# A hybrid decoder trunk: the attention of the first layer with VectorE and ScalarE, too, in a written order

## The chip, the core and the metric

The kernel runs on one core of a Trainium2 chip. The metric is the time of one execution on the device, in microseconds (us), as the median of several runs. TensorE does the matrix products, VectorE (DVE) and ScalarE (ACT) read their results out of PSUM, GpSimd (POOL) works on SBUF, and SyncE (SP) issues the DMA transfers.

## The reference

A trunk of two layers over 1024 tokens of width 1024, in float32. Layer 0, which the change touches, is

```python
h = rmsnorm(x, attn_norm[0])
q_a, k_a, v_a, q_b, k_b, v_b = split(h @ w_in)
o_a = stick_breaking_attention(q_a, k_a, v_a)          # 8 heads x 64, strictly causal
o_b = sliding_window_attention(q_b, k_b, v_b, sinks, rel_bias_table)   # 8 q heads, 2 kv heads, window 128
x = x + concat(o_a, o_b) @ w_out
x = x + swiglu(rmsnorm(x, ffn_norm[0]), ...)
```

In stick-breaking attention a weight is `exp(log_beta + between)`, where `between` is a reversed cumulative sum of `log_sigmoid(-z)` over the keys; the kernel forms it as a running product of `sigmoid(-z)` along reversed keys, and the weights are its differences, which it moves into the values. In sliding-window attention the scores get a relative bias and each head a sink, and a softmax follows. Layer 1 has latent attention and the same kind of feed-forward block; a final normalisation ends the trunk.

## The kernel before

Everything is kept as transposed tiles of 128 features by 512 tokens; `hf` names the half of the tokens. A float32 operand is split into a high part (`hi`, rounded by a ScalarE cast) and the rest (`lo`, a VectorE subtraction), and a product is three matrix products (`mm3`). Weights come through `stream`: `take()` returns a unit, and sees to it that the next one is loaded (DMA into `wa`) and split (`whi` on ScalarE, `wlo` on VectorE, four buffers each), a whole unit of up to two tiles at a time.

`layer0_attention` projects the first pair of stick-breaking heads, and then calls `weave`, which interleaves eight segments with filler. The first four segments are the four pairs of stick-breaking heads (20 slots each), the other four the pairs of sliding-window heads (8 slots each). A slot holds, in this order of emission:

- `part`: transposes of two blocks of weights into a PSUM bank `t` (two buffers), and their split into `pth` (ScalarE) and `ptl` (VectorE);
- the scores that the slot two ahead needs (`AHEAD`): the product into a bank `z`; then for stick-breaking a sigmoid on ScalarE into `w` and a scan on VectorE (L683, L685), for sliding-window a bias addition (L589) and a maximum (L591) on VectorE and two exponentials on ScalarE (L593), after GpSimd has put the sink beside them (L588);
- filler: quarters of the projections of the next pair (`unit_items`: 24 products in four parts, evacuated by VectorE into `ev` at L507 and then stacked by `stack_q`, `stack_k` or turned into value tokens by `sb_values` and `v_tokens`), the rows of the relative bias, and in the last four segments the early output projection (`early_out`, L835) with its reloads. How much of it a slot takes is its share of the segment's weight; it is used up one slot before the segment's end;
- the product with the values (`pv`, bank `o`) of the slot before, and, where a group of blocks ends, `end`: a copy of half the bank (`otmp`, ScalarE) and additions on VectorE (L725, L626).

At the end of a half, sliding-window outputs are multiplied by the reciprocal sums (`normalise`: a transpose, a copy `rrow`, a round trip through memory, a GpSimd multiplication at L331), and `done` stores the split output (`spill`: cast L312, GpSimd subtraction L313, two DMAs). `early_out` reads the stick-breaking outputs back (`early_act`, L827). The bias rows of a pair of sliding-window heads are read (L574) when its first block is scored.

Who sets the order: the block of `weave` stands in

```python
with self.tc.manual_schedule(engines={mybir.EngineType.PE}):
```

so TensorE executes it as it is written. The instructions of VectorE, ScalarE, GpSimd and SyncE are ordered by a planner that simulates the program, with its own costs. Every engine takes its instructions in the order so found and waits on semaphores for what is not ready.

## Time and profile before

| | before |
|---|---|
| median of three runs | 2510.03 us (2509.27 to 2511.41) |
| profiled execution | 2502.03 us, span 2500.3 us |
| granted TensorE clock, mean | 0.972 |
| busy: TensorE, VectorE, ScalarE, GpSimd | 93%, 77%, 49%, 39% of the span |
| stick-breaking part of the weave | 63.8 to 351.4 us, TensorE busy 263.54 us |
| sliding-window part | 351.4 to 493.0 us, TensorE busy 128.15 us |

In a row of the timeline stand the start, the duration, the engine, the line, the operation with output and inputs by their names, and in brackets the idle time of that engine before it with what ended it. A row of the waits has the engine and line that waited, what it waited for, the total in us, the number of times and the longest.

### The profile page before, as it was taken

What the parts mean: (1) busy time and instruction counts of PE and PEld (TensorE: products, weight loads), DVE (VectorE), ACT (ScalarE), POOL (GpSimd) and SP (SyncE); (2) the same over time, 40 slices, a digit from 0 to 9 for tenths busy, and PEclk for the clock granted to TensorE, in tenths of its full rate; (3) what the DMA queues carried; (4) which work ended last, traced back from release to release, by engine and by line L of the source; (5) the groups of instructions that cost most, each with busy time, mean ns of one, the idle gap of its engine ahead of it and who ended that gap; (6) DMA issues with size and microseconds to landing.
All of it is one profiled execution on the core that took longest, in us unless ns stands there. A gap on an engine that the chain in (4) does not pass through costs nothing. (4 is left out here: it accounts for less than half of the span.)

```text
span 2500.3 us, 33743 instructions
## 1 busy us (share of the span) xinstructions
PE 2334.6 (93%) x11252; PEld 1913.9 (77%) x11252; DVE 1912.7 (77%) x2864; ACT 1237.0 (49%) x2469; POOL 979.4 (39%) x786
## 2 busy tenths in 40 slices
PE   7999999888999999899987999999989999998996
PEld 4777787776788888678766888887768888886784
DVE  6777776779676667799977888885588766678988
ACT  5555555554233334344655787774453333343453
POOL 5333232216975354343222323321047544533333
PEclk9999999999999999999998999999989999999998
DMA  3011225543444234453333111135225433345531
GB/s 119 26 43 39 68 99 192 189 171 122 141 137 140 88 107 151 145 171 123 121 115 95 50 62 60 53 133 195 90 96 183 146 105 102 107 129 170 169 103 71
DMA packets 161931, 289.22 MB, mean 116 GB/s; under 512 B 20091, under 2 KB 28764, under 8 KB 161756
## 3 DMA queue, kind: packets, MB, share of 16 engines
q1 hardware_dynamic: 161756, 287.05, 35.1%
q8 instruction: 89, 1.46, 0.2%
q14 instruction: 86, 0.70, 0.1%
HBM read 207.19 MB, written 79.27 MB: 115 GB/s over the span
## 5 line engine op out<-in xcount | busy, mean ns | idle before, releaser
L145 ACT CAST whi<-wa 128x512 fp32r<-128x512 f32 (+1 forms) x422 | 255.8, 607 | 473.3 <-PE mm L231 118.8
L146 DVE TENSOR_TENSOR wlo<-wa,whi 128x512 fp32r<-128x512 f32 (+1 forms) x422 | 334.0, 792 | 63.9 <-ACT whi L145 62.2
L177 POOL TENSOR_TENSOR wa<-s,wa 128x512 f32<-128x512 f32 (+1 forms) x68 | 97.0, 1426 | 327.1 <-DVE wlo L146 297.8
L195 POOL TENSOR_TENSOR s<-wb,wb 128x512 f32<-128x512 f32 (+1 forms) x68 | 104.6, 1538 | 161.6 <-DVE wlo L146 146.2
L146 DVE TENSOR_TENSOR wlo<-wb,whi 128x512 fp32r<-128x512 f32 (+1 forms) x136 | 136.2, 1001 | 33.3 <-ACT whi L145 33.2
L1424 PE MATMUL z<-mk,mq 128*128 128x512 f32 (+2 forms) x576 | 148.1, 369 | 11.2 <-ACT w L1437 10.4
L145 ACT CAST whi<-wb 128x512 fp32r<-128x512 f32 (+1 forms) x136 | 82.3, 605 | 142.3 <-PE a L231 43.6
L230 PE MATMUL mm<-hh,whi 128*128 128x512 f32 x312 | 129.0, 413 | 1.7 <-ACT whi L145 1.7
L1437 ACT ACTIVATE w<-z,st 128x512 f32<-128x512 f32 (+3 forms) x192 | 110.9, 583 | 35.3 <-DVE st L1433 25.4
L231 PE MATMUL mm<-hl,whi 128*128 128x512 f32 x312 | 125.6, 403 | 0.0
L177 POOL TENSOR_TENSOR wa<-wa,wa 128x512 f32<-128x512 f32 (+1 forms) x68 | 100.0, 1471 | 65.3 <-issue 52.0
L232 PE MATMUL mm<-hh,wlo 128*128 128x512 f32 x312 | 125.4, 402 | 0.0
L1430 DVE TENSOR_REDUCE st<-z 128x1 f32<-128x512 f32 (+1 forms) x192 | 104.2, 550 | 26.8 <-PE z L1424 19.1
L391 DVE TENSOR_TENSOR ptl<-t,pth 128x512 fp32r<-128x512 f32 x160 | 108.2, 684 | 18.2 <-ACT pth L390 13.5
L927 POOL TENSOR_TENSOR c<-c,c 128x512 f32<-128x512 f32 x66 | 99.3, 1518 | 43.1 <-DVE c L1031 37.1
L1424 PEld LDWEIGHTS z<-mk,mq 128*128 128x128 f32 x576 | 93.4, 194 | 24.7 <-ACT w L1437 16.2
L177 POOL TENSOR_TENSOR wb<-wa,wb 128x512 f32<-128x512 f32 (+1 forms) x68 | 101.9, 1499 | 3.5
L390 ACT CAST pth<-t 128x512 fp32r<-128x512 f32 x160 | 91.1, 590 | 19.0 <-PE t L387 8.0
L395 PE MATMUL mm<-pth,v 128*128 128x256 f32 x320 | 94.6, 312 | 2.9 <-ACT pth L390 2.8
L387 PE MATMUL t<-ident,w 128*128 128x128 f32 x576 | 94.8, 277 | 1.3 <-ACT w L1437 1.2
L395 PE MATMUL mm<-ptl,v 128*128 128x256 f32 x320 | 88.0, 299 | 2.0 <-DVE ptl L391 2.0
L703 DVE TENSOR_TENSOR ptl<-t,pth 128x512 fp32r<-128x512 f32 x80 | 54.4, 683 | 41.0 <-ACT pth L702 40.5
(526 smaller groups left out, 7640.4 us busy)
## 6 DMA issues: line engine op xcount, KB each, us to landing
a<-c SPq DMA_DIRECT2D x124, 256.0 KB, 2.1
ld<-a SPq DMA_DIRECT2D x98, 256.0 KB, 3.7
wa<-w_gate SPq DMA_DIRECT2D x60, 256.0 KB, 2.7
wa<-w_up SPq DMA_DIRECT2D x60, 256.0 KB, 2.6
lone<-a SPq DMA_DIRECT2D x56, 256.0 KB, 3.3
wb<-w_gate SPq DMA_DIRECT2D x44, 256.0 KB, 2.9
wb<-w_up SPq DMA_DIRECT2D x44, 256.0 KB, 2.8
wa<-w_in SPq DMA_DIRECT2D x36, 256.0 KB, 2.6
```

Of the source, the lines that this page charges most:

```text
L145: nc.scalar.copy(hi[:, :n], raw[:, :n])
L146: nc.vector.tensor_tensor(lo[:, :n], raw[:, :n], f(hi[:, :n]), ALU.subtract)
L177: sub = lambda o, x, y: nc.gpsimd.tensor_tensor(o, x, y, ALU.subtract)
L195: nc.gpsimd.tensor_tensor(s1, a21, a22, ALU.add)
L230: mm(ps, wh, xh, start=first, stop=False)
L231: mm(ps, wh, xl, start=False, stop=False)
L232: mm(ps, wl, xh, start=False, stop=last)
L391: nc.vector.tensor_tensor(lo, t, f(hi), ALU.subtract)
L395: nc.tensor.matmul(o[:, :256], vs, pt[:, j * 256:(j + 1) * 256], start=(kb == kb0 and j == 0 and i == 0), stop=(kb == NB - 2 and j == 1 an ...
L1424: nc.tensor.matmul(z[:, :wd + ext], qq[:, q0:q0 + P], kk[:, k0 - ext:k0 + wd], start=y == 0, stop=y == 2 and x > 0)
L1430: nc.vector.tensor_reduce(st[:, x:x + 1], zs[x], AX.X, ALU.max, negate=True)
L1437: nc.scalar.activation(w[:, o:o + wd], zs[x], AF.Exp, bias=st[:, 2 * np_ - 2:2 * np_ - 1], accum_out=box[p]["s"][c // 2][:, 8 * x + j:8 * ...
```

## The change

VectorE and ScalarE join TensorE in the written order. So that an engine does not stand before work that depends on something just issued, `defer` puts that work off by one to four slots; `put_off` emits what is due in each slot, after the slot's own work and ahead of its filler. In a slot the scores for two slots ahead now come first, then the transposes, then the second halves (scans or exponentials), then `lo`. The filler is used up two slots before a segment's end. `woven_stream` splits one tile at a time between the filler's parts. The bias rows of the next pair are read at the sixth block of the pair before, and every second set has the tile `unseen` for a home, which stick-breaking no longer uses then.

```diff
+        def load(i):
+            raws[i] = []
+            for src, n in parts(i):
+                raw = self.tl(self.wp, [P, HALF], F32, "wa", 4)
+                self.nc.sync.dma_start(out=raw[:, :n], in_=src)
+                raws[i].append((raw, n))
+        def step():
+            for i in range(len(ready), min(take.i + 2, len(units))):
+                if i not in raws:
+                    load(i)
+            i = len(ready)
+            if i <= take.i and i < len(units):
+                take.part.append(self.split_w(*raws[i][len(take.part)]))
+                if len(take.part) == len(raws[i]):
+                    ready.append(take.part)
+                    take.part = []
+        def take():
+            while len(ready) <= take.i:
+                step()
+            take.i += 1
+            return ready[take.i - 1]
+        take.i, take.part, take.step, take.ready = 0, [], step, ready
+        return take
...
-            if k % 2 and k < nk - 1:
-                yield
+            if k % 2:
+                self.w_take.step()
+                if k < nk - 1:
+                    yield
...
+    def defer(self, n, fn):
+        if self.slot_now is None:
+            fn()
+        else:
+            self.deferred.append((self.slot_now + n, fn))
     def weave(self, segments):
         AHEAD = 2
-        slots, seg_of = [], []
+        slots = []
         for seg, filler in segments:
-            total, n, done = sum(w for w, _ in filler), sum(len(st[1]) for st in seg), 0
+            total, n, i = sum(w for w, _ in filler), sum(len(st[1]) for st in seg), 0
             run = (g for w, fn in filler for g in self.weighted(fn, w))
-            i = 0
-            for scores, parts, end in seg:
+            for scores, parts in seg:
                 base = len(slots)
-                for j, part in enumerate(parts):
+                for part in parts:
                     i += 1
-                    slots.append({"t": part, "z": [], "run": run, "quota": total * i / (n - 1),
-                                  "end": end if j == len(parts) - 1 else None, "last": i == n, "seg": len(seg_of)})
+                    slots.append({"part": part, "need": [], "run": run, "quota": total * i / (n - 2), "last": i == n})
                 for need, fn in scores:
-                    slots[base + need].setdefault("need", []).append(fn)
-            seg_of.append(0)
-        zs = [[] for _ in slots]
-        for i, sl in enumerate(slots):
-            zs[max(i - AHEAD, 0)] += sl.get("need", [])
-        pending, used, cur = [], 0, None
-        for i, sl in enumerate(slots):
-            if i == 0:
-                first = zs[0]
-                zs[0] = []
-                for fn in first:
-                    fn()
-            pv = sl["t"]()
-            for fn in zs[i]:
+                    slots[base + need]["need"].append(fn)
+        for fn in [fn for sl in slots[:AHEAD] for fn in sl["need"]]:
+            fn()()
+        self.deferred, pv, used, cur = [], None, 0, None
+        for self.slot_now, sl in enumerate(slots):
+            nxt = slots[self.slot_now + AHEAD:self.slot_now + AHEAD + 1]
+            rest = [fn() for x in nxt for fn in x["need"]]
+            lo, pv_next = sl["part"]()
+            for fn in rest + [lo]:
                 fn()
+            self.put_off(self.slot_now)
             if sl["run"] is not cur:
                 cur, used = sl["run"], 0
             while used < sl["quota"] or sl["last"]:
                 if next(cur, None) is None:
                     break
                 used += 1
-            for fn in pending:
-                fn()
-            pending = [pv] + ([sl["end"]] if sl["end"] else [])
-        for fn in pending:
-            fn()
+            if pv:
+                pv()
+            pv = pv_next
+        pv()
+        self.put_off(None)
+        self.slot_now = None
+    def put_off(self, now):
+        while True:
+            due = [x for x in self.deferred if now is None or x[0] <= now]
+            if not due:
+                return
+            self.deferred.remove(due[0])
+            due[0][1]()
...
+            def part(h=h, m=m, l=l):
+                nc.scalar.copy(khs[h][m, c], src[m, :])
+                nc.scalar.copy(khs[h][l, c], src[m, :])
+                nc.gpsimd.tensor_tensor(kls[h][m, c], src[m, :], f(khs[h][m, c]), ALU.subtract)
+                nc.gpsimd.tensor_tensor(kls[h][l, c], src[m, :], f(khs[h][m, c]), ALU.subtract)
+            self.defer(h, part)
...
-            rest = fn(self.evac(ps, hf), hf, box["t"])
-            if rest is not None:
-                yield from rest
+            t = self.evac(ps, hf)
+            self.defer(1, lambda: fn(t, hf, box["t"]))
...
-            if b == 0:
-                box["b"] = self.tl(self.atp, [P, HALF], F32, "u", 3)
-                for h in range(2):
-                    rows = self.dram("bias", 2 * mi + h, width=WLEN + 1)
-                    nc.sync.dma_start(out=box["b"][:, 256 * h:256 * h + 256],
-                                      in_=bass.AP(rows.tensor, rows.offset + P - 1, [[WLEN, P], [1, 256]]))
-            bias = box["b"].rearrange("p (h k) -> p h k", h=2)
+            if mi == b == 0:
+                bias_rows(0)
+            if b == 5 and mi < 3:
+                bias_rows(mi + 1)
+            bias = self.bias[mi].rearrange("p (h k) -> p h k", h=2)
...
             box["p", b] = pt, o
+            def exps():
+                for h in range(2):
+                    nc.scalar.activation(pt[:, h, o:], pt[:, h, o:], AF.Exp, bias=st[:, h:h + 1],
+                                         accum_out=box["s", b // 4][:, h, b % 4:b % 4 + 1])
+            return exps
...
-            nc.vector.tensor_tensor(lo[:, :n], t[:, :n], f(hi[:, :n]), ALU.subtract)
-            return lambda: pv(b, nk, hi, lo)
+            return (lambda: nc.vector.tensor_tensor(lo[:, :n], t[:, :n], f(hi[:, :n]), ALU.subtract),
+                    lambda: pv(b, nk, hi, lo))
...
+            self.defer(1, lambda: end(b, o))
+        def end(b, o):
+            if b % 4 == 0:
+                box["o"] = self.tl(self.atp, [P, HALF], F32, "o", 3)
+            ot = box["o"]
...
-                self.normalise(box["s", hf].rearrange("p h b -> p (h b)"), hf, ot, "u", 3)
-                done(hf, ot)
-        return [([(0, lambda b=b: score(b))], [lambda b=b: part(b)], None) for b in range(NB)]
+                sums = box["s", hf].rearrange("p h b -> p (h b)")
+                nc.vector.reciprocal(sums, sums)
+                self.defer(1, lambda: self.normalise(sums, hf, ot, "u", 3, True))
+                self.defer(4, lambda: done(hf, ot))
...
+            self.defer(2 - i, lambda d=d, i=i: self.v_tokens(d, i, box["v"]))
...
+            def scan():
+                if first:
+                    nc.vector.tensor_tensor_scan(u[:, :w], u[:, :w], self.unseen[:, :w], 1.0, ALU.mult, ALU.max)
+                else:
+                    nc.vector.tensor_tensor_scan(u[:, :w], u[:, :w], u[:, :w], prev, ALU.mult, ALU.bypass)
+            return scan
...
+            return lambda: nc.vector.tensor_tensor(lo, t, f(hi), ALU.subtract), lambda: pv(h, c, kb, hi, lo)
...
+            if kb == NB - 2:
+                self.defer(1, lambda o=box["ps"]: end(h, c, o))
...
-                done(c // 2, box["o"][c // 2])
+                self.defer(1, lambda: done(c // 2, box["o"][c // 2]))
...
-            self.w_take = self.stream(units + outs[12:])
             pre = [[], []]
-            self.w_take.loaded.extend(pre)
+            self.w_take = self.woven_stream(units + outs[12:], pre)
+            self.slot_now, self.bias = None, {}
...
-            with self.tc.manual_schedule(engines={mybir.EngineType.PE}):
+            with self.tc.manual_schedule(engines={mybir.EngineType.PE, mybir.EngineType.Activation, mybir.EngineType.DVE}):
```

More of the change, by code (lines that the diff above doesn't have):

```diff
@@ L169, in stream, with woven_stream, parts @@
         return take
+    def woven_stream(self, units, split):
+        units, ready, raws = list(units), list(split), {}
+        def parts(i):
+            src, n = units[i]
+            return [(src[:, c:min(c + HALF, n)], min(HALF, n - c)) for c in range(0, n, HALF)]
+        def load(i):
[21 more added lines that the diff above has]
+        return take
     def forms(self, mats):
@@ L551, in sw_v_tokens @@
         nc = self.nc
-        yield
         t = self.bank("t")
@@ L565, in swa_steps, with bias_rows @@
         box = {}
+        def bias_rows(i):
+            t = self.tl(self.atp, [P, HALF], F32, *(("unseen",) if i % 2 else ("u", 3)))
+            self.bias[i] = t
+            for h in range(2):
+                rows = self.dram("bias", 2 * i + h, width=WLEN + 1)
+                nc.sync.dma_start(out=t[:, 256 * h:256 * h + 256],
+                                  in_=bass.AP(rows.tensor, rows.offset + P - 1, [[WLEN, P], [1, 256]]))
         def score(b):
@@ L681, in score @@
             nc.scalar.activation(u[:, :w], z[:, ext:ext + w], AF.Sigmoid, scale=-0.125)
[L682 to L685 removed]
+            prev = box.get(key)
             box[key] = u[:, w - 1:w]
@@ L745, in step @@
             scores.sort(key=lambda x: x[0])
-            return scores, [lambda kb=kb: part(h, c, kb, rows) for kb in range(2 * c, NB, 2)], lambda: end(h, c)
+            return scores, [lambda kb=kb: part(h, c, kb, rows) for kb in range(2 * c, NB, 2)]
         return [step(h, c) for h, c in order]
```

38 lines of the change are left out of this document (10 added, 28 removed).

## The prediction

> **What bounds the kernel now.** I read the page first, then stretches of the span stage by stage, then TensorE's waits in the changed stage, and last the timeline of each kind of wait. A row of a stretch gives the busy time of each engine and, behind them, the granted clock.
>
> ```profile
> PE 2334.6 (93%) x11252; PEld 1913.9 (77%) x11252; DVE 1912.7 (77%) x2864; ACT 1237.0 (49%) x2469; POOL 979.4 (39%) x786
> ...
> 63.80:351.40 287.60, 263.54 (x1469) 223.51 (x1467) 217.92 (x326) 157.34 (x320) 92.38 (x75) 0.96 0.13 44
> 351.40:493.00 141.60, 128.15 (x711) 110.42 (x710) 101.61 (x208) 86.87 (x236) 39.76 (x52) 0.95 0.60 196
> ...
> 130.00:145.00 15.00, 11.44 (x55) 9.32 (x54) 9.25 (x16) 5.56 (x14) 2.94 (x3) 0.77 0.14 53
> 200.00:215.00 15.00, 11.42 (x59) 9.34 (x58) 9.89 (x18) 6.31 (x14) 2.99 (x4) 0.89 0.15 53
> 270.00:285.00 15.00, 11.04 (x40) 6.85 (x39) 10.41 (x24) 7.20 (x17) 2.48 (x3) 0.77 0.20 69
> ...
> PE t L699 <- DVE v L370: 10.7, 4, 3.3
> PE t L604 <- ACT w L593: 10.5, 5, 4.6
> PE t L699 <- DVE w L683: 5.7, 9, 1.6
> PE t L555 <- DVE ev L507: 2.5, 2, 1.3
> ```
>
> TensorE sets the time. The changed weave has two stages: stick-breaking (63.8 to 351.4 us, 80 slots) and sliding-window (to 493.0, 32 slots). TensorE idles 24.1 us in the first and 13.5 us in the second, and runs part of both at a reduced clock: 4% of 287.6 is 11.5 us, 5% of 141.6 is 7.1 us. That is 56 us, the most that any order could give. The last four rows (us, times, longest) name most of the idle time.
>
> **What the old orders of VectorE and ScalarE cost.** First a stick-breaking slot, then the end of a pair of heads and the seam to the next.
>
> ```profile
> 103.58 0.69 DVE L703 TENSOR_TENSOR ptl<-t,pth 128x512 fp32r<-128x512 f32 x1 [1.94 <-ACT pth L702]
> 104.19 3.03 DVE L683 TENSOR_TENSOR_SCAN w<-w,unseen 128x512 f32<-128x512 f32 x2
> ...
> 107.27 0.33 PE L699 MATMUL t<-ident,w 128*128 128x128 f32 x1 [0.55 <-DVE w L683]
> ...
> 128.12 0.28 PE L712 MATMUL o<-pth,v 128*128 128x256 f32 x1
> ...
> 128.59 0.60 PE L699 MATMUL t<-ident,w 128*128 128x128 f32 x4
> 128.95 0.72 PE L679 MATMUL z<-qk,qk 128*128 128x256 f32 x4
> ...
> 134.33 2.59 DVE L683 TENSOR_TENSOR_SCAN w<-w,unseen 128x512 f32<-128x512 f32 x2
> 136.84 1.59 DVE L370 TENSOR_TENSOR v<-t,v 128x256 fp32r<-128x256 f32 x4
> 138.24 0.45 PE L699 MATMUL t<-ident,w 128*128 128x128 f32 x1 [2.34 <-DVE v L370]
> ```
>
> In the slot, VectorE stands idle 1.94 us because a `ptl` subtraction, which nobody needs yet, is ahead of two scans; TensorE then waits for the scans. The given order puts the scans of slot i+2 ahead of `lo` of slot i, so the scans run while ScalarE casts `hi`. At the seam four `v` subtractions run together behind two scans, and both `t` banks hang on them.
>
> Now a sliding-window seam (first VectorE, then ScalarE, then SyncE's queue):
>
> ```profile
> 385.19 0.69 DVE L589 SCALAR_TENSOR_TENSOR w<-z,u 128x512 f32<-128x512 f32 x1 [3.60 <-PE o L621]
> 385.80 0.68 DVE L835 TENSOR_TENSOR w<-w,mm 128x512 f32<-128x512 f32 x1
> 386.40 0.68 DVE L591 TENSOR_REDUCE sst<-w 128x2 f32<-128x514 f32 x1
> ...
> 387.59 0.57 DVE L626 TENSOR_TENSOR o<-o,otmp 64x128 f32<-64x128 f32 x2
> ...
> 384.04 0.62 ACT L312 CAST oh<-o 128x512 fp32r<-128x512 f32 x1 [3.43 <-POOL o L331]
> 384.56 0.61 ACT L145 CAST whi<-wa 128x512 fp32r<-128x512 f32 x1
> ...
> 387.11 0.51 ACT L593 ACTIVATE w<-w,sst 128x257 f32<-128x257 f32 x1 [1.15 <-DVE sst L591]
> ...
> 388.23 0.37 ACT L624 COPY otmp<-o 64x256 f32<-64x256 f32 x1
> ...
> 381.19 0.43 SPq L574 DMA_DIRECT2D u<-bias  x1
> ```
>
> VectorE's bias addition waits until 385.19 though its `z` was done; the named releaser is not it, but the bias rows, issued only at 381.19. ScalarE meanwhile stands behind a cast that waits for GpSimd's multiplication.
>
> **The change part by part.** The sum is against the profiled execution: 2502.03 us (span 2500.3), 8.0 us below the median of 2510.03; differences carry over.
>
> *Stick-breaking, inside a pair.* Scans ahead of `lo`, `z` ahead of `t`, projection work cast a slot after its evacuation: the 5.7 and 2.5 us of the last two waits should nearly go. VectorE's 217.92 us over 80 slots is 2.7 us a slot against about 3.2 of TensorE, so an order with one slot of slack can hold. I leave 1.0 us: -7.2 us.
>
> *Its three inner seams.* They cost now 3.56 + 3.58 + 3.96 us idle and 15 x (0.23 + 0.11 + 0.23) = 8.6 us of clock: 19.7. The filler now ends two slots before the seam (quota over n-2), and these slots have on TensorE only PV products (0.47, from 128.12 to 128.59), `t` (0.36, to 128.95), one `v` transpose (as `t`) and `z` (0.72 for two narrow ones, some 1.0 for two wide): 0.47 x 2 + 0.36 x 3 + 1.7 = 3.7 us. VectorE's list there is an evacuation (0.6), scans of 256, 128 and twice 512 (about 1.4 and 2.2, more beside GpSimd), two `lo` (1.2), two `v` subtractions (0.8) and one end (0.6): 6.8. The first transposes of the next pair need the bank that this list frees last. So 3.0 us of idling per seam stays (6.8 - 3.7, rounded; bounds 0 if the backlog is absorbed, 3.7 as now), and with it a clock loss, for which I take the mildest of the rows, 0.11 x 15 = 1.65. That is 4.65 x 3 = 14.0, thus -5.7 us. The start of the weave keeps its order: 0.
>
> *Sliding-window.* Bias rows are asked for at b=5 of the group before, some five slots early, and `done` comes four slots late: the 10.5 us wait and the ScalarE block go, and SyncE, idle between, hides the 8 issues that move ahead of others. But a new ring appears. In each slot VectorE adds the bias and reduces, ScalarE exponentiates, then copies `otmp`, then VectorE adds two halves, and only then takes the next slot's bias addition. From the rows: 0.60 (bias addition, start to next start) + 0.71 (386.40 to 387.11) + 1.12 (387.11 to 388.23) + 0.40 (`otmp`) + 0.57 (at 387.59) = 3.4 us. `lo` hides in it; the rest does not: per group 6 `wlo`, 4 residual additions, 2 evacuations at 0.6 each, and ahead of `otmp` 4 stack casts and 2 `oh` casts at 0.62: 10.9. Eight slots make 27.2 + 10.9, about 38 us. TensorE's own work is less:
>
> ```profile
> 351.40:387.70 36.30, 33.49 (x194) 29.08 (x192) 25.01 (x50) 22.21 (x60) 11.06 (x15) 1.00 0.54 185
> 387.70:425.60 37.90, 35.09 (x190) 30.08 (x190) 26.81 (x55) 23.23 (x64) 12.62 (x16) 0.95 0.50 163
> 425.60:465.50 39.90, 35.06 (x190) 30.21 (x190) 26.64 (x55) 23.34 (x64) 11.88 (x14) 0.94 0.73 237
> 465.50:493.00 27.50, 24.51 (x137) 21.05 (x138) 23.14 (x51) 18.09 (x53) 4.19 (x7) 0.90 0.62 195
> ```
>
> These are the four groups; less the clock's share (as 0.05 x 37.9) they are 33.5, 33.2, 32.7 and 21.8 us. So groups 2 and 3 go from 37.9 and 39.9 to 38 each, bound by the ring. Group 4 has six ring slots (20.4), two short ones (3.2), 4 additions, 3 `wlo`, 2 casts (5.4) and a backlog of about 1: 30 against 27.5.
>
> Group 1 gets a wait of its own. The last stick-breaking output must be stored and read back for the early output projection:
>
> ```profile
> 358.34 0.62 ACT L312 CAST oh<-o 128x512 fp32r<-128x512 f32 x1
> ...
> 360.37 0.33 SPq L315 DMA_DIRECT2D ol<-o  x1
> ...
> 364.08 0.43 SPq L827 DMA_DIRECT2D qk<-ol  x1
> ...
> 367.60 0.39 PE L230 MATMUL mm<-qk,whi 128*128 128x512 f32 x1
> ...
> DMA to landing us min/median/max: 3.2/3.2/3.2
> ```
>
> The last read lands at 367.3, the product starts at 367.6: no slack now. The cast moves from the start of slot 1 to the middle of slot 2 (end one slot later, `done` another), some 6 us, behind that slot's exponentials, while the product stays 16 us after the stage's start. Some 2 us are found by the need for k=3 only late in the first unit: 4 us stay (0 to 6). The first group is then 33.5 + 4 = 37.5. Stage: 37.5 + 38 + 38 + 30 = 143.5, plus two clock losses of 1.65, 146.8 against 141.6: +5.2 (bounds: -13 with no ring, +10 with it everywhere).
>
> *Weight splits one tile at a time.* As many casts and subtractions as before; loads are asked for a unit ahead, some six slots, against 2 to 4 us of landing. 0; if that cover went, a landing per unit.
>
> *The tail.* `done` of group 4's first half comes after the last slot. From the copy of its sums to its cast now:
>
> ```profile
> 486.03 0.26 ACT L324 COPY rrow<-t 8x128 f32<-8x128 f32 x1
> ...
> 493.41 0.62 ACT L300 CAST hh<-o 128x512 fp32r<-128x512 f32 x1 [1.70 <-POOL o L331]
> ```
>
> 7.4 us; the copy now falls in slot 6, with two short slots and nine products of cover. 0 to 4.5; I take +1, as the planner may put other products ahead.
>
> Sum: -7.2 - 5.7 + 5.2 + 1 = -6.7 us: profiled 2495.3, median **2503**. On queues that the change leaves to the planner (GpSimd, SyncE) the steps only move.
>
> The Trainium skill, page "TensorE: Matmul & The Clock Gate", in the table at its head, says that ScalarE and VectorE take their queues in strict order. The trace agrees (the `whi` cast at 384.56 follows the `oh` cast that had waited 3.43 us); it speaks against a written order wherever a wait is misjudged, as in the ring.
>
> **The rivals.**
> - *No ring* (0.22): `otmp` and the additions find gaps. For it: the old order held 27.5 us for eight slots of group 4. Against: the given order allows no overtaking. Sliding-window is then 121.2 + 4 + 3.3 = 128.5, -13.1: in all 2485.
> - *The clock stays up* (0.10): gaps of 3 us leave it alone. Against it: 2.34 us at 138.24 came with 0.77. Without the losses, 5.0 + 3.3 us less: 2495. The same page, "HAM oscillation", sets the limit at an idle window of some 3.4 us; by that rule the clock holds, but the 2.34 us row speaks otherwise.
> - *GpSimd's queue* (0.20, slower): a group's sink copy (`w`, L588) stands behind the multiplication by the sums, which waits for a round trip through memory.
>
> ```profile
> POOL o L331 <- DMA u<-rrow: 22.6, 7, 7.7
> ```
>
>  Seven waits of 3.2 us, plus 1.3 us of work. VectorE's reduction needs the sink; in a written order all of VectorE then stands. With the ring there is no slack to hide it. If half of eight times 4.5 us shows, +18: 2521. It decides once the sink copy comes later than its bias addition.
> - *Nothing gained* (0.15): the waits taken out of stick-breaking come back as others at half their size, and the ring takes the rest: 2510.
>
> **How the numbers follow.** Forecast 0.33, own range 2496 to 2511. A difference of 0.2% (5 us) is about what this kernel's runs can tell. Faster: 0.20 of the forecast, 0.10 and 0.22: 0.52. Same: 0.11 of the forecast and 0.12 of the last rival: 0.23. Slower: 0.20 and what is left of both: 0.25. The range runs from just under "no ring" to "GpSimd's queue": 2482 to 2521.
>
> **What would show it.** Right: `t` <- `w` L683 near nothing in stick-breaking; at 130 to 285 us gaps of some 3 us before the first `t` of a pair, behind `ptl`; no wait for `bias`; in sliding-window VectorE idle before `o` <- `otmp` once a slot, about 1 us, and TensorE waiting for `w` exponentials every eight slots; a wait of `mm` <- `qk` in group 1. Wrong: sliding-window groups under 36 us (no ring), or VectorE waiting for the sink copy.

## The result: slower by 1%, and where the profile after puts it

The median of four runs is 2534.64 us (2530.57 to 2537.79) against 2509.65 us before in the same series: a ratio of 1.0098, interval 1.0081 to 1.0116. The forecast of 2503 was wrong, and so was its sign. The profiled execution has a span of 2532.7 us against 2500.3, 32.4 us more; the profiled execution of before lay 8 us under its median, hence more than the 25 us of the medians.

Four marks cut the span alike in every kernel here: the first stick-breaking transpose `t`, the first and last sliding-window transpose, and the first cast of `B11h` in the next part. Of the 32.4 us, -1.7 lie before the first mark, -1.5 in stick-breaking (280.3 to 278.8), +25.2 in sliding-window (139.3 to 164.5), +9.4 from its last transpose to that cast (48.8 to 58.2) and +1.0 in all that follows. So a large loss and a tail; the 1.5 us of stick-breaking are less than one profile can tell (see below the table). First the stretches of the changed kernel as the prediction cut them; the granted clock is the third figure from the end.

```profile
63.10:348.30 285.20, 267.46 (x1473) 225.73 (x1471) 218.36 (x322) 155.31 (x316) 91.40 (x74) 0.95 0.13 42
348.30:385.80 37.50, 34.03 (x163) 27.45 (x164) 23.98 (x44) 19.30 (x52) 8.95 (x12) 0.91 0.47 157
385.80:426.00 40.20, 34.12 (x186) 28.93 (x185) 26.71 (x51) 21.05 (x60) 10.99 (x15) 0.96 0.38 124
426.00:470.00 44.00, 36.40 (x182) 30.76 (x181) 28.22 (x52) 21.11 (x57) 12.59 (x14) 0.88 0.61 203
470.00:513.00 43.00, 32.21 (x172) 26.93 (x170) 32.12 (x64) 25.07 (x70) 7.67 (x12) 0.88 0.57 179
```

In stick-breaking TensorE's idle time fell from 24.1 to 17.7 us, but its busy time for the same products rose by 3.9. In sliding-window both rose: idle from 13.5 to 28 us, busy from 128.15 to 136.76, at a clock of 0.88 to 0.96. TensorE's waits over the weave, and below them VectorE's longest in the second stage:

```profile
PE t L361 <- DVE sum L698: 11.5, 3, 6.7
PE t L766 <- DVE ptl L770: 8.4, 4, 2.7
PE o L682 <- DVE o L693: 7.3, 6, 2.9
PE mm L266 <- ACT whi L145: 6.4, 2, 3.5
PE t L668 <- DVE ptl L673: 5.2, 3, 2.6
PE mm L267 <- DMA qk<-ol: 3.4, 3, 1.9
...
PE o L778 <- DVE ptl L770: 1.6, 3, 0.5
PE t L402 <- DVE u L718: 1.2, 3, 0.4
...
DVE o L693 <- ACT otmp L691: 36.9, 28, 2.6
```

The waits for scans and evacuations inside a pair are gone, and so is the one behind the bias rows. New, or grown, are the waits for `sum` (the end of sliding-window), for additions (L693), for weight casts and for `ol`, the stored output, and the 28 waits of VectorE for the copy `otmp` (36.9 us; before, 6 waits and 10.1 us). One turn of that ring, VectorE first, then ScalarE, then TensorE:

```profile
403.79 0.68 DVE L649 SCALAR_TENSOR_TENSOR w<-z,unseen 128x512 f32<-128x512 f32 x1
404.57 0.69 DVE L651 TENSOR_REDUCE sst<-w 128x2 f32<-128x514 f32 x1
...
408.12 0.58 DVE L693 TENSOR_TENSOR o<-o,otmp 64x128 f32<-64x128 f32 x2 [2.27 <-ACT otmp L691]
408.74 0.69 DVE L560 TENSOR_TENSOR ev<-mm,r 128x512 f32<-128x512 f32 x1
409.35 0.68 DVE L649 SCALAR_TENSOR_TENSOR w<-z,unseen 128x512 f32<-128x512 f32 x1
...
405.30 0.51 ACT L656 ACTIVATE w<-w,sst 128x257 f32<-128x257 f32 x1 [1.11 <-DVE sst L651]
...
406.44 1.26 ACT L568 CAST qk<-ev 64x512 fp32r<-64x512 f32 x2
407.72 0.37 ACT L691 COPY otmp<-o 64x256 f32<-64x256 f32 x1
...
414.19 0.80 PE L266 MATMUL mm<-qk,whi 128*128 128x512 f32 x1 [3.51 <-ACT whi L145]
```

From one bias addition to the next pass 5.56 us: bias addition and maximum, the exponentials that wait for it, two stack casts, the copy, the additions that wait for the copy, an evacuation. One turn later TensorE stands 3.51 us before a weight cast that ScalarE reaches only behind all this.

### The profile page after: what moved, and what is told of

It reads as the page before. It is cut to its first block, busy times and chain, and to the rows that moved or that the text cites. A ratio compares the mean times of both kernels' runs of the same rounds, so it can differ in the third digit from the quotient of the medians.

```text
span 2532.7 us, 33661 instructions
## 1 busy us (share of the span) xinstructions
PE 2348.9 (93%) x11252; PEld 1920.7 (76%) x11252; DVE 1921.4 (76%) x2864; ACT 1236.7 (49%) x2469; POOL 978.7 (39%) x786
## 5 line engine op out<-in xcount | busy, mean ns | idle before, releaser
L146 DVE TENSOR_TENSOR wlo<-wa,whi 128x512 fp32r<-128x512 f32 (+1 forms) x422 | 341.4, 812 | 58.6 <-ACT whi L145 56.7
L1498 DVE TENSOR_REDUCE st<-z 128x1 f32<-128x512 f32 (+1 forms) x192 | 104.0, 549 | 25.2 <-PE z L1492 17.9
L430 DVE TENSOR_TENSOR ptl<-t,pth 128x512 fp32r<-128x512 f32 x160 | 108.0, 682 | 16.1 <-ACT pth L429 14.3
L1492 PEld LDWEIGHTS z<-mk,mq 128*128 128x128 f32 x576 | 92.6, 192 | 23.9 <-ACT w L1505 15.4
L939 POOL TENSOR_TENSOR acc<-acc,sq 128x512 f32<-128x512 f32 x26 | 35.9, 1381 | 129.5 <-ACT sq L934 129.4
```

The source lines that it names most:

```text
L146: nc.vector.tensor_tensor(lo[:, :n], raw[:, :n], f(hi[:, :n]), ALU.subtract)
L430: nc.vector.tensor_tensor(lo, t, f(hi), ALU.subtract)
L1492: nc.tensor.matmul(z[:, :wd + ext], qq[:, q0:q0 + P], kk[:, k0 - ext:k0 + wd], start=y == 0, stop=y == 2 and x > 0)
L1498: nc.vector.tensor_reduce(st[:, x:x + 1], zs[x], AX.X, ALU.max, negate=True)
```

## The experiments

In the table the second column is the ratio to the kernel before, run beside it on the same chip, with its interval; the others are one profile's distances between the marks (us).

| kernel | ratio | stick-breaking | sliding-window | to the cast |
|---|---|---|---|---|
| before | 1 | 280.3 | 139.3 | 48.8 |
| after | 1.0098 (1.0081 to 1.0116) | 278.8 | 164.5 | 58.2 |
| tail_order | 1.0067 (1.0042 to 1.0092) | 276.6 | 162.7 | 52.8 |
| pe_only | 0.9945 (0.9921 to 0.9969) | 275.8 | 135.7 | 52.1 |
| pe_dve | 0.9990 (0.9967 to 1.0013) | 278.2 | 135.6 | 59.4 |
| pe_act | 1.0063 (1.0042 to 1.0084) | 273.8 | 158.5 | 54.1 |
| otmp_first | 1.0028 (1.0007 to 1.0049) | 274.3 | 146.9 | 58.1 |
| sb_three | 0.9959 (0.9937 to 0.9981) | 279.2 | 135.0 | 50.0 |
| before_bias | 0.9947 (0.9914 to 0.9980) | 279.4 | 130.4 | 49.5 |
| pe_tail | 0.9937 (0.9910 to 0.9964) | | | |
| seam_lo | 0.9961 (0.9942 to 0.9980) | 276.8 | 135.7 | 49.6 |
| seam_filled | 0.9956 (0.9936 to 0.9977) | 277.4 | 138.1 | 50.0 |
| mended | 1.0009 (0.9989 to 1.0029) | 272.0 | 145.4 | 53.0 |
| rows_later | 0.9941 (0.9918 to 0.9963) | 276.7 | 135.4 | 49.4 |
| before_rows | 0.9985 (0.9971 to 1.0000) | 284.9 | 131.4 | 49.5 |
| mended_rows | 0.9998 (0.9981 to 1.0016) | 271.5 | 143.8 | 52.4 |
| hybrid | 0.9948 (0.9928 to 0.9967) | 275.2 | 134.1 | 48.8 |
| mended_quota | 0.9931 (0.9904 to 0.9959) | 277.2 | 134.1 | 52.2 |
| mended_act_free | 0.9956 (0.9940 to 0.9973) | 277.2 | 134.2 | 51.5 |
| mended_sb_only | 0.9935 (0.9909 to 0.9960) | 276.5 | 134.2 | 49.6 |

How sure the columns of one profile are: after, tail_order, otmp_first and sb_three run stick-breaking in one and the same order, and lie from 274.3 to 279.2; so do mended, mended_quota, mended_act_free and mended_sb_only, and lie from 272.0 to 277.2. A difference of some 5 us in that column says nothing by itself. In sliding-window pe_only, sb_three, seam_lo, seam_filled and rows_later have one order, and lie from 135.0 to 138.1. What follows the last mark is the same work in every kernel, and takes from 1956.2 us (before_bias) to 1971.3 (seam_lo) in these profiles.

**Which engine's order costs.**

```
-with self.tc.manual_schedule(engines={PE, Activation, DVE}):
+with self.tc.manual_schedule(engines={PE}):              # pe_only
+with self.tc.manual_schedule(engines={PE, DVE}):         # pe_dve
+with self.tc.manual_schedule(engines={PE, Activation}):  # pe_act
```

> The changed kernel with TensorE alone in the written order, VectorE and ScalarE left to the planner; deferral, early bias rows and single-tile splits stay. Theory (the loss is the ring of VectorE and ScalarE in the sliding-window stage, and the tail): that stage comes back from 167 us to 140 or less (bias rows early), the tail to what it was, stick-breaking stays between 285 and 290 us: 2500 to 2508. Rival (the new order of TensorE, filler used up two slots early, is what costs): sliding-window stays over 155 us, 2525 or more. Second rival (the lower clock after the seams is the loss): 2520, with the clock of 0.5 to 0.75 still at 135, 205 and 275 us.

> The changed kernel with TensorE and VectorE in the written order, ScalarE left to the planner. Theory: the ring needs both engines, since the copy of half the bank must stand behind the exponentials; with ScalarE free that copy is placed as soon as its bank is done, and half or more of the loss goes: 2510 to 2520. Rival (VectorE's order alone closes the ring: it stands before the additions until the copy has come, whoever orders that): within 5 us of the changed kernel, 2530 or more.

> The changed kernel with TensorE and ScalarE in the written order, VectorE left to the planner. Theory: the planner puts the next bias addition ahead of the additions that wait for the copy, so the ring opens: 2505 to 2518, sliding-window stage under 150 us; the tail, whose wait is on ScalarE, stays long (8 us). Rival (ScalarE's order is the one that costs, by casts that wait for GpSimd and weight casts behind the exponentials): 2528 or more.

TensorE's new order alone is faster than before; it isn't what costs. With VectorE written too, sliding-window stays at 135.6 us; with ScalarE written too, it takes 158.5. So it is ScalarE's order. That contradicts my expectation for pe_act: I had thought that freeing VectorE would open the ring. The planner did put bias additions ahead of the additions there, and VectorE's waits for the copy fell from 36.9 to 14.3 us; but the copy still comes late, and TensorE waits 9.4 us for the additions behind it (L693), which release the bank `o`, and 4.6 for weight casts. In pe_dve the planner puts the copy ahead of the stack casts, and a weight cast ahead of both:

```profile
398.04 0.62 ACT L145 CAST whi<-wa 128x512 fp32r<-128x512 f32 x1 [0.47 <-PE mm L267]
398.80 0.37 ACT L691 COPY otmp<-o 64x256 f32<-64x256 f32 x1
399.07 1.26 ACT L568 CAST qk<-ev 64x512 fp32r<-64x512 f32 x2
```

The tail, against what I expected, goes with VectorE's order: 59.4 us in pe_dve, 54.1 in pe_act.

**The copy by itself.**

```
+for fn in self.firsts: fn()          # nc.scalar.copy(tmp, o[64:128, :256])
 for fn in rest + [lo]: fn()          # exponentials, lo
```

> The changed kernel, written order on all three engines, with one thing moved: in the sliding-window slots ScalarE's copy of half the bank (otmp) is emitted ahead of the slot's exponentials instead of behind them; VectorE's additions stay where they are. Theory (what closes the ring is this one place in ScalarE's order: the copy waits for exponentials, these for VectorE's bias addition, and that for the additions that need the copy): the sliding-window stage falls from 164 us, first to last transpose, to 145 or less, the idle time of VectorE before the additions goes, and the whole to 2508 to 2518. Rival (it is ScalarE's other work, casts that wait for GpSimd's multiplication and weight casts behind the exponentials): the stage stays over 155 us, 2525 or more.

164.5 falls to 146.9 us, and VectorE's waits for `otmp` in this stage, 36.9 us in the changed kernel, leave the list. The ring was shut at that one place. But 12 us more than with the planner stay, a little more than I had allowed, and the tail is untouched.

**The tail.** In the changed kernel (ScalarE, VectorE, TensorE):

```profile
519.47 0.62 ACT L338 CAST hh<-o 128x512 fp32r<-128x512 f32 x1 [5.47 <-POOL o L370]
...
520.12 0.69 DVE L339 TENSOR_TENSOR hl<-o,hh 128x512 fp32r<-128x512 f32 x1 [5.51 <-ACT hh L338]
...
521.93 0.20 DVE L698 RECIPROCAL sum<-sum 128x8 f32<-128x8 f32 x1
...
522.19 0.37 PE L361 MATMUL t<-ident,sum 128*8 128x128 f32 x1 [6.66 <-DVE sum L698]
```

The cast `hh` of the first half waits for a round trip through memory, and VectorE's subtraction `hl` for `hh`. The copies (ScalarE), additions and the reciprocal (VectorE) of the second half, which need nothing of it, stand behind these two. That it is VectorE's place that counts, pe_dve shows: there ScalarE makes the copies at 486.27 and 486.94, but VectorE still stands before `hl`, with the additions and the reciprocal behind it, and TensorE waits 8.2 us for the sums.

```profile
492.98 0.69 DVE L339 TENSOR_TENSOR hl<-o,hh 128x512 fp32r<-128x512 f32 x1 [7.03 <-ACT hh L338]
```

One line empties the list by due slot:

```
-due = [x for x in self.deferred if now is None or x[0] <= now]
+due = sorted(..., key=lambda x: x[0] if now is None else 0)
```

> The changed kernel, except that what is still put off after the last slot is emitted in the order of its due slots: the ends of the last two blocks first, then the sums' normalisation, then the storing of both halves. Theory: the storing of the first half stands at the head of that list and its cast waits 5.5 us on ScalarE for a round trip through memory, with the last copies, additions and the second half's normalisation behind it; TensorE waits 6.7 us for the sums at 522. So the tail loses some 7 to 8 us: 2527. Rival: the round trip itself sets the end, whoever stands behind it: within 2 us of the changed kernel, 2533 or more.

> TensorE alone in the written order, and what is put off after the last slot emitted by due slot. Theory: with the planner free to order VectorE and ScalarE the order of emission in the tail still sets priorities and TensorE's own order: 1 to 4 us below TensorE alone, the time from the last transpose to the next stage down from 52 to 49 us. Rival: the planner had already moved the tail's work, no difference.

That wait of TensorE falls from 6.66 to 1.35 us, the stretch from 58.2 to 52.8. In the whole time the gain isn't shown, since the intervals of the two ratios overlap. With TensorE alone written (pe_tail) the step from pe_only, 0.9945 to 0.9937, is inside the intervals, too, and its stretch stays unread.

**One part alone: the bias rows.** The kernel before, with `bias_rows(mi + 1)` at the sixth block and nothing else of the change:

> The kernel before, with one part of the change alone: the bias rows are read at the sixth block of the pair before, into the second home. Theory (the wait for the rows stood alone, 3.3 to 4.6 us at each of three seams): the waits of TensorE for the exponentials at the seams go, sliding-window some 5 to 9 us shorter, 2501 to 2505. Rival (ScalarE stands there just as long behind the cast that waits for GpSimd): within 3 us of before.

Sliding-window falls from 139.3 to 130.4 us (131.4 in before_rows, which has the same early load), TensorE's waits for the exponentials there from 10.5 to 6.1 us, and the ratio to 0.9947. The two profiles differ by 13.8 us in all; 4.5 of these lie behind the last mark, where nothing was changed. No kernel here has an interval that lies below this one's: all that any of them can be shown to gain, the bias rows alone bring.

**Stick-breaking: written or planned.** All three engines written for 80 slots, TensorE alone behind:

> The changed kernel with all three engines in the written order for the 80 stick-breaking slots and TensorE alone from there on. Theory (the written order of VectorE and ScalarE brings stick-breaking nothing that TensorE's order does not bring alone): within 5 us of the kernel with TensorE alone, 2497 to 2507. Rival (it does help there, as predicted, and its gain was only covered by the later loss): 3 to 8 us below TensorE alone, 2491 to 2496.

0.9959 against 0.9945 for TensorE alone: the orders of VectorE and ScalarE bring stick-breaking nothing that these runs can tell. Why not, when TensorE's waits inside the pairs went? The seam between two pairs, as sb_three has it, first VectorE, then TensorE:

```profile
131.91 2.34 DVE L759 TENSOR_TENSOR_SCAN w<-w,unseen 128x512 f32<-128x512 f32 x2
134.28 0.69 DVE L778 TENSOR_TENSOR ptl<-t,pth 128x512 fp32r<-128x512 f32 x1
...
135.03 0.48 PE L774 MATMUL t<-ident,w 128*128 128x128 f32 x1 [2.69 <-DVE ptl L778]
```

The stretches behind it (length and busy time first, the clock third from the end):

```profile
135.00:140.00 5.00, 4.70 (x15) 3.69 (x16) 3.04 (x7) 3.16 (x7) 1.28 (x1) 0.50 0.28 105
140.00:145.00 5.00, 5.00 (x26) 4.18 (x26) 1.98 (x3) 1.82 (x4) 0.00 (x0) 0.89 0.33 105
```

The rule "scans ahead of `lo`" helps in every slot but this: here the scans are the next pair's, which nobody needs yet, and TensorE waits 2.69 us for the `lo` behind them. Behind it its clock is 0.50 for the first stretch and 0.89 in the second: 2.5 and 0.55 us lost. Two experiments, one that moves the wait's cause and one that only fills the wait:

```
+if sl["last"] and self.slot_now < 79:      # seam_lo
+    lo(); self.put_off(self.slot_now); lo = lambda: None
...
+if self.slot_now in (20, 40, 60):          # seam_filled
+    d = self.bank("mm")
+    for x in range(24): self.nc.tensor.transpose(d[...], self.ident, self.ident)
```

> As the kernel sb_three (all three engines in the written order for stick-breaking, TensorE alone behind it), with one thing moved: in the last slot of each of the first three pairs VectorE subtracts lo, and takes what is put off, ahead of the scans of the next pair instead of behind them. Theory (at a seam nobody needs these scans yet; TensorE's 2.69 us wait for ptl is just the 2.34 us of two 512-wide scans that the written order put ahead, and the clock falls after the wait): the waits at the three seams fall from 2.7 us to about 1, the clock in the 15 us behind them stays nearer to 1, stick-breaking 5 to 14 us shorter than the 274 to 279 us of all kernels with this order. Rival (the backlog of VectorE is what it is, and the wait moves to the value transposes): under 3 us.

> As sb_three, with 24 transposes of the identity, which nobody reads, put on TensorE at each of the three inner seams, where it waits 2.69 us for ptl: the work is as before, only the wait is filled (24 at 0.09 us, 2.2 us). Theory (the idle time itself brings the clock down): the clock behind the seams stays at 1.00 where it was 0.5 to 0.75, and each seam gains the 3 us that its products lose at the low clock: stick-breaking 270 us or less, 6 to 10 us less in all. Rival (the clock falls for another reason, the bursts of scans or the products' kind): clock and time as in sb_three, or up to 3 us longer where the filling doesn't fit the gap.

seam_lo, TensorE at the same seam, and below it the stretch behind:

```profile
132.37 0.33 PE L778 MATMUL t<-ident,w 128*128 128x128 f32 x1 [0.32 <-DVE ptl L782]
...
133.65 0.63 PE L402 MATMUL t<-ident,u 128*128 128x128 f32 x4 [0.67 <-DVE v L409]
```

```profile
135.00:140.00 5.00, 5.00 (x28) 4.25 (x28) 4.47 (x7) 2.24 (x6) 0.73 (x1) 1.00 0.17 61
```

seam_filled, the same two views:

```profile
132.94 2.79 PE L537 MATMUL mm<-ident 128*128 128x128 f32 x24
135.78 0.33 PE L778 MATMUL t<-ident,w 128*128 128x128 f32 x1
```

```profile
135.00:140.00 5.00, 4.27 (x26) 3.40 (x25) 3.42 (x8) 3.15 (x7) 1.29 (x1) 1.00 0.28 105
```

Both keep the clock at 1.00 there. In seam_filled the transposes of the next pair come no earlier than in sb_three (2.96 us behind the last product, 2.97 there); TensorE has only been busy meanwhile. So it was the idle time that brought the clock down. Yet neither the totals (0.9961, 0.9956) nor the stage (276.8 and 277.4 us, where some 10 less had been expected) differ from sb_three by more than the scatter. At the third seam both lose their clock again: seam_filled behind a wait of 1.26 us for the bias rows' tile `u`, seam_lo behind one of 1.87 for `ptl`. Of seam_lo the first products of the bias rows, and two stretches:

```profile
268.54 2.92 PE L471 MATMUL mm<-w,u 33*128 33x384 f32 x4 [0.98 <-DVE u L467]
```

```profile
275.00:280.00 5.00, 5.00 (x16) 3.30 (x14) 1.89 (x5) 2.44 (x6) 1.00 (x1) 0.50 0.50 184
...
285.00:290.00 5.00, 5.00 (x10) 2.83 (x11) 1.38 (x2) 1.89 (x4) 0.00 (x0) 0.50 0.36 120
```

There TensorE is busy all the time and stays at half clock. The filler after this seam is the bias rows' products, on 33 of 128 rows. They were suspected, and moved behind the keys' projection, in three kernels:

```
-fill = [..., self.bias_items() + k + qs[0][0] + v, ...
+fill = [..., k + self.bias_items() + qs[0][0] + v, ...
```

> As seam_lo, with one thing moved: in the fourth pair's filler the products of the bias rows (eight times four products on 33 of 128 rows) come behind the projection of the keys instead of ahead of it, so that dense products follow the third seam as they do the first two. Theory (the clock, once down, does not come up under these thin products, though TensorE is busy all the time): behind the third seam it stays near 1, the 20 us at 0.5 go, stick-breaking 8 to 10 us shorter than in seam_lo, 266 to 269 us, 2488 to 2493 in all. Rival (the third seam has a longer wait and its clock falls with that): the low clock stays for 10 us or more, under 4 us gained.

> The kernel before with early bias rows (before_bias) and the products of the bias rows behind the keys' projection; no written order of VectorE or ScalarE. Theory (thin products hold the clock down): at 270 to 290 us the planner's seam loses 3.4 us of clock in before; 1 to 3 us of them come back, 2495 to 2499, a little under before_bias. Rival: no difference from before_bias, or up to 3 us more, as the rows come later in memory.

> The kernel mended (three engines in the written order throughout, four places mended), with the bias rows' products behind the keys' projection. Theory: stick-breaking 4 to 8 us shorter than the 272 us of mended; sliding-window keeps its 145 us, since nothing is moved there: 2500 to 2507, a little under before. Rival: what is gained before 350 us is lost again to the sliding-window order, 2508 to 2512.

The stretches of rows_later:

```profile
270.00:275.00 5.00, 5.00 (x28) 4.25 (x27) 4.94 (x9) 3.06 (x8) 0.53 (x1) 1.00 0.32 105
...
290.00:295.00 5.00, 4.82 (x15) 3.09 (x14) 2.90 (x9) 2.31 (x6) 0.68 (x1) 0.50 0.23 80
```

The seam now keeps its clock, and the drop to 0.50 went with the rows to 290 us, behind a wait of 1.55 us for `u`. Stick-breaking gained nothing (276.7 against 276.8, and 271.5 in mended_rows against 272.0 in mended), and before_rows came out at 284.9, no better than before_bias. So moving the thin products moves the loss, and the 8 to 10 us didn't come. That these products hold the clock down, as the theory had it, isn't shown: in the kernel before it is back at 1.00 among the same products, 9 us after a wait of 2.72 us at 276.30.

```profile
285.00:290.00 5.00, 5.00 (x26) 3.27 (x25) 4.19 (x9) 3.67 (x8) 0.91 (x1) 1.00 0.75 262
```

Whether the rows, their waits or something else keeps it down so long in seam_lo stays open.

**Can a fully written order work?** First with four places mended (the copy, the tail, `lo` at the seams, the last pair's output stored a slot earlier):

> The changed kernel, all three engines in the written order throughout, with four places of the order mended: the copy otmp ahead of the exponentials, what is put off after the last slot by due slot, lo ahead of the scans at the seams, and the last pair's stick-breaking outputs stored a slot earlier. Theory (these four places are the loss): 17 us from the copy, 9 from the tail, 5 to 14 from the seams, 2 from the store: 2495 to 2505, level with TensorE alone. Rival (a written order of three engines keeps a cost that no single place carries, since nothing may overtake): 2510 or more, sliding-window still over 142 us.

1.0009: the rival was right in its numbers, level with before, with sliding-window at 145.4. Its reason, a cost that no single place carries, doesn't hold, as the next kernels show. TensorE's waits in it:

```profile
PE t L678 <- DVE ptl L683: 7.1, 4, 2.2
PE mm L266 <- ACT whi L145: 2.5, 2, 1.3
```

Then, on top of mended, three ways to find the rest (the last two edits in short):

```
-"quota": total * i / (n - 2)
+"quota": total * i / (n - (2 if n == 20 else 1))       # mended_quota
...
+if self.slot_now == 80: engines={PE, DVE}               # mended_act_free
+if self.slot_now == 80: engines={PE}                    # mended_sb_only
```

> As mended, with the sliding-window filler used up one slot before the end of each group, as in the kernel before, instead of two. Theory (the last two of eight slots hold no products of the filler, so that TensorE has some 1.7 us of work a slot there against 2.7 of VectorE, and waits for ptl at 411, 451 and 466 us): 1 to 2 us less at each group, sliding-window 138 to 141 us, 2503 to 2507. Rival (the waits sit at the groups' seams whatever the filler does): 143 us or more, level with mended.

> As mended, with ScalarE left to the planner from the first sliding-window slot on, VectorE and TensorE written. Theory (what remains is ScalarE's order: weight casts and storing casts behind each slot's exponentials): sliding-window 134 to 138 us, as with the kernel pe_dve, 2498 to 2504. Rival (VectorE's written order keeps its part now that the copy no longer explains it): 142 us or more.

> As mended up to the last stick-breaking slot, TensorE alone in the written order from there on. Theory (the stages add): stick-breaking 272 to 275, sliding-window 134 to 136, tail as with TensorE alone: 2488 to 2496, the least of the kernels with the new order of TensorE. Rival (what stick-breaking gains comes back at its end, since the store and the reading back of its last output set the start of the early output projection): 2497 to 2501.

mended_quota, with all three engines written to the end, has 0.9931, as good as any kernel here; the two inner groups of its sliding-window stage have no idle time left:

```profile
378.00:414.00 36.00, 36.00 (x209) 31.07 (x208) 28.33 (x58) 24.06 (x65) 12.03 (x17) 1.00 0.50 158
414.00:450.00 36.00, 35.98 (x205) 30.78 (x204) 28.56 (x59) 24.29 (x68) 12.89 (x17) 1.00 0.79 266
```

So the other place was the filler's end: of eight slots two had none of its products, and there TensorE waited for `ptl` (7.1 us in mended, 0.8 here). My expectation for the quota, 138 to 141 us, was too small an effect. The copy (164.5 to 146.9) and the filler's end (145.4 to 134.1) make 28.9 us together, as much as the changed kernel loses against those with TensorE alone written (135 to 136). Freeing ScalarE instead (mended_act_free) brings the same 134.2 us with the filler as it was, and so does freeing both (mended_sb_only): the thin slots cost only where ScalarE's order is written. What exactly the planner does otherwise there wasn't traced. mended_sb_only, expected to be the least of all, can't be told from the others.

Last, stick-breaking from the written order and sliding-window in the order of before with early rows:

> Stick-breaking as in rows_later (three engines in the written order, seams mended, rows behind the keys), sliding-window in the order of before (TensorE alone written, nothing put off, filler to one slot before the end) with the early bias rows, tail by due slot. Theory (the stages add): stick-breaking 267, sliding-window 130 to 132 as in before_bias, the rest as in before: 10 to 13 us under before_bias, 2486 to 2490. Rival (the gain in stick-breaking comes back later, through a tail or a start of the sliding-window stage that waits): 2495 to 2500, level with before_bias.

0.9948, level with before_bias, as the rival had it. Neither stage reached what the theory asked of it, 275.2 us where 267 and 134.1 where 130 to 132 stood; why sliding-window takes longer than in before_bias isn't shown. mended_quota, mended_sb_only, pe_tail and before_bias can't be told apart by their intervals; each of these lies under 1, hence under both kernels of this case.

## Why the prediction was wrong, step by step

The step that failed most is the sliding-window stage: +5.2 us forecast, +23.1 found by the prediction's stretches (141.6 to 164.7) and +25.2 between the marks. The tail is next (+1 against +9.4), then stick-breaking (-12.9 against -2.4).

- *Stick-breaking, inside a pair* (-7.2): right. The waits for `w` and `ev` are gone. Without the seams and the start's 3.1 us, idle time in the stage fell from 9.9 to 3.1 us (24.1 - 11.1 - 3.1, and 17.7 - 11.5 - 3.1), of which 1.6 is a new wait of `o` for `ptl`: -6.8.
- *Its three inner seams* (-5.7): wrong in both terms. The long wait was right, 2.69 us where 3.0 stood, three times. Left out were the short ones beside it, for `u` (1.2 and 0.4), `v` (0.8) and the bias rows (1.0): 11.5 us of idling against 9.0 predicted and 11.1 before. And the clock: I took the mildest row, 1.65 us a seam. In the written order (sb_three's rows) the first seam loses 2.5 us at 135 to 140 and 0.55 up to 145, and the third more, 6.8 us from 270 to 290. Busy time in the stage rose by 3.9 us where 3.6 less had been predicted: that is 7.5 of the 10.5 us by which -12.9 became -2.4, and the seams' idling is 2.5. The short waits, in the waits of the changed kernel up to 349 us:

```profile
PE mm L471 <- DVE u L467: 1.0, 1, 1.0
...
PE t L402 <- DVE v L409: 0.8, 3, 0.3
PE t L402 <- POOL u L716: 0.4, 1, 0.4
```

- *Sliding-window* (+5.2): the ring was rightly found and, for groups 2 and 3, rightly sized. Taking the clock's share off each stretch as the prediction did leaves 34.1, 38.6, 38.7 and 37.8 us against 37.5, 38, 38 and 30. Two terms failed: the clock, 3.3 predicted and 15.4 found (0.09 x 37.5 + 0.04 x 40.2 + 0.12 x 44 + 0.12 x 43), since slow products follow the long waits (3.51 us at 414.19, then 0.75 from 415 to 420; 2.94 at 457.97, then 0.50 from 460 to 465); and group 4, 7.8 us more than its ring. Group 1 came out 3.4 us shorter than forecast; its wait for `ol` is there, 3.4 us where 4 stood.
- *What the sum left out*: the filler ending two slots early was counted for stick-breaking only. In sliding-window it thins two slots of eight; with the ring open that cost 11 us (145.4 to 134.1). No term of the sum stands for it.
- *Weight splits* (0): wrong. The cover named was the early load; what went was ScalarE's freedom to cast before the exponentials. TensorE waited 6.4 us for `whi`, where the prediction had looked for waits on the exponentials.
- *The tail* (+1, at most 4.5): 9.4 us. The step looked at the round trip alone, not at what stands behind the cast `hh` on ScalarE and, above all, behind `hl` on VectorE. Emptying the list by due slot brought 5.4 us back.
- *The bias rows*: right, their wait is gone, and alone they give 8.9 us.
- *The rivals*: "GpSimd's queue" came nearest in time, at 2521, but VectorE never waited for the sink copy. "The clock stays up" is refuted by the 0.50 behind 2.69 us. The rule in the Trainium skill, page "TensorE: Matmul & The Clock Gate", in the table at its head, that ScalarE and VectorE take their queues in strict order lies under the ring; the rows shown agree (the copy of 407.72 follows the casts of 406.44, and the additions of 408.12 wait 2.27 us for it with the next evacuation behind them).

## What to carry to other kernels

An order written for three engines is only as good as its worst single place: here one copy behind two exponentials was worth 17 us of its stage, filler that ended one slot too early 11, and one list emptied in the wrong order 5, while its good parts brought nothing that could be measured. Before taking an engine's order from the planner, write down for each instruction what it waits for and what stands behind it, at the seams and the end above all, and test each part of such a change alone: the one that paid was an early load that needed no written order. A price for a wait of TensorE should include the slow products behind it, here some 3 us for 2.7. And before believing a stage's gain, look at how far the same order scatters from one profile to the next: here 5 us.

## What the runs showed of the hardware

- Behind a wait of 2.69 us, in a stretch from 130 to 135 in which TensorE was busy for 1.91 us, the granted clock fell to 0.50; with the same wait filled by 24 transposes that nobody reads, or cut into 0.32 and 0.67 us, it stayed at 1.00. Waits of 1.24 and 1.33 us, at 389.40 and 391.17 in the changed kernel, left it at 1.00 up to 400. The Trainium skill, page "TensorE: Matmul & The Clock Gate", section "HAM oscillation", gives idle gaps of over some 3.4 us as the limit; the rows here speak for less.
- Busy isn't enough: between 275 and 290 us TensorE had no idle time in seam_lo and a clock of 0.50, where products of 33 rows took 2.9 us of each 5 to 6. It recovered some 4 us into the dense products behind them. In before it recovered among the same products.
- In the clock record of the traces the low clock lasts for whole steps of 3.41 us: 6.8 us behind each of the first two seams of sb_three and behind the third of before, 23.9 behind the third of seam_lo, none behind the first two of seam_lo and seam_filled.
- Two 512-wide scans that took 2.34 us (131.91) took 3.39 in seam_lo at 133.42, where a GpSimd subtraction ran beside them, itself 2.08 us long where sb_three has 1.28:

```profile
133.42 3.39 DVE L763 TENSOR_TENSOR_SCAN w<-w,unseen 128x512 f32<-128x512 f32 x2
...
133.64 2.08 POOL L351 TENSOR_TENSOR o<-o,oh 128x512 f32<-128x512 f32 x1 [4.29 <-ACT oh L350]
```

The Trainium skill, page "SBUF — State Buffer", section "SBUF: two separate sides", says that such a VectorE operation with two SBUF inputs and GpSimd share a port pair that one of them holds for a whole instruction; the two rows agree. The first of the two scans took 1.22 us, about half of 2.34; the subtraction, begun 0.22 us after it, is 0.80 longer, and the second scan, which ends at 136.81, some 1.0, as if each had waited for the one before it to end.
